# A two-layer hybrid decoder trunk: the operands of its Strassen products are prepared later in VectorE's queue, and its first weight is rounded earlier in ScalarE's

## The chip, the cores and the metric

The kernel runs on one core of one Trainium2 chip. TensorE (PE) multiplies matrices, VectorE (DVE) and ScalarE (ACT) work on rows of 128 partitions, GpSimd (POOL) does a few additions and subtractions, and SyncE (SP) and ScalarE issue the DMAs. The metric is the device time of one execution in microseconds (us); lower is better. Times are medians of the runs shown.

## The reference

Two pre-norm layers over 512 positions of width 1024, and a final norm. Each layer computes, from the normed input, a stick-breaking attention (four heads), a dilated attention (three groups of four heads, with partial rotary), two gates, merges the two branches and projects; then a gated feed-forward block with a convolution of width 3 follows. Cut to what the change touches:

```
h = rms_norm(x, norm_mix)                        # x: 512 x 1024
u = h @ w_in                                     # q, k, v of both attentions, and the gates
# stick-breaking, per head, t = query, s = key:
z = (q @ k.T) / 8
log_keep = where(s < t, log_sigmoid(-z), 0)
suffix   = reverse_cumsum(log_keep) - log_keep
A = where(s < t, exp(log_sigmoid(z) + suffix), 0)
yb = A @ v
# dilated attention: three groups (window, dilation), merged by their softmax denominators
```

## The kernel before

**Precision and weights.** Every float32 product is made of three products of rounded halves: with `hi` the rounded and `lo` the rest, `hi*h + hi*l + lo*h`. The weights stream in from memory in tiles `raw` of 512 KB (L290, issued by SyncE, five buffers); ScalarE writes `hi` (L299) and VectorE `lo = raw - hi` (L300) into a ring of twelve buffers. The same is done for activations: `xh` (L218) and `xl` (L219) for the normed input, `Bh` (L374) and `Bl` (L375) for the right operands below. Squares of x (L229, L232) serve the norm's root mean square, which is applied after the projections as `r` (`rbc`) or `rt` (`ny`).

**A layer's first part.** In this order of the program: the norm's splits and squares; a value projection, `vproj` (L344, four accumulators `acc` in PSUM, evicted by ScalarE at L347); the stick-breaking q and k, `sb_qk` (L320 to L322; each has two halves, so there are four evictions `sbq` in a layer, by VectorE, L591); a second, late value projection, whose four results ScalarE evicts into `stg` (L347) and eight DMAs on ScalarE's queue and eight on SyncE's scatter by residue (L352). All of these share four `acc` banks, so a projection cannot start before an older result in its bank is evicted. Then comes the stick-breaking attention itself, `sb_pair` (`z`, `e`, `sp`, `sh`: L500 to L538), mixed with the dilated projections.

**Right operands and Strassen products.** The dilated projections and the gates use a seven-product scheme of the Strassen kind on halves of the matrices. `hx` (L611, VectorE, eight times) scales x in place by the gain and the norm. `b_ops` then forms the operands named "11", "1", "2", "3", "21", "22" and "4": sixteen differences of half tiles on POOL (L405, written to `x` or to `T`), each split by ScalarE into `Bh` and by VectorE into `Bl`, and the four lower tiles split as they are (`plain`, 512 wide). `strassen` adds and subtracts blocks of a weight on POOL and VectorE (POOL: L427, L430, L440; VectorE: L431) and multiplies. The first product goes to a bank X, which ScalarE evicts as p1 into `s` (L429) before the fifth product may go on in X:

```
sprod(X, wsplit(a11), BT, "11", True)
S.activation(p1, X, AF.Copy)                 # L429
...
sprod(Y, wsplit(a11), BT, "2", True)
sprod(Z, wsplit(S1), BT, "1", True)
sprod(W, wsplit(a21), BT, "3", True)
sprod(X, wsplit(a12), BT, "21", False)
```

**What sets the order.** The program is written as above, but a scheduler places the instructions on each engine by its own model of their times; each engine then runs its queue strictly in order. `tc.issue_after(ins)` adds to what is written in its block the condition that it stands behind `ins`.

Of the kernel before, what the change touches and what calls it, by code (L numbers as in the profile page):

```python
# [13 lines left out]
AF = mybir.ActivationFunctionType  # L14
ALU = mybir.AluOpType
# [6 lines left out]
KD = 8  # L22
# [94 lines left out]
def trunk(ctx: ExitStack, tc: tile.TileContext, xt_d, pos_d, cst_d, vec_d, w_d, out_d):  # L117
    nc = tc.nc
    V, S, G, PE = nc.vector, nc.scalar, nc.gpsimd, nc.tensor
# [95 lines left out]
    def norm_split(k, gcol, st):  # L215
        h, lo = bslot_r("xh"), bslot_r("xl")
        g = vec[:, gcol + k:gcol + k + 1]
        S.activation(h, x[k], AF.Copy, scale=g)  # L218
        V.scalar_tensor_tensor(lo, x[k], g, h.bitcast(F32), op0=ALU.mult, op1=ALU.subtract)  # L219
        st["x", k] = (h, lo)  # L220
# [4 lines left out]
    def sq_sum(k, st):  # L225
        a = st.setdefault("a", [])
        if k < 2:
            a.append(scratch("sqa"))
            S.activation(a[k], x[k], AF.Square)  # L229
        else:  # L230
            q = temp("sq", tag="ta")
            S.activation(q, x[k], AF.Square)  # L232
            (V if k % 2 else G).tensor_tensor(a[k % 2], a[k % 2], q, ALU.add)  # L233
# [20 lines left out]
        V.scalar_tensor_tensor(y, t, 1.5, y, op0=ALU.add, op1=ALU.mult)  # L254
        return y

    last_row, last_num, last_out = [None], [None], [None]
    last_b = []

    def r_rows(y, n):  # L260
# [15 lines left out]
    def wraw(what, between=None):  # L276
        l, i = divmod(wpos[0], len(plan))
        wpos[0] += 1
        assert plan[i][0] == what
        n, out = plan_cols(plan[i]), []  # L280
        for c in range(0, n, 1024):
            e = min(n, c + 1024)
            raw = wp.tile([128, 1024], F32, tag="raw", name=nm("raw"), bufs=NRAW)
            o = int(offs[i]) + c
            if between and c == 0:
                nc.sync.dma_start(raw[:, :512], w_d[l, :, o:o + 512])
                between(0)
                nc.sync.dma_start(raw[:, 512:], w_d[l, :, o + 512:o + 1024])
            else:
                nc.sync.dma_start(raw[:, :e - c], w_d[l, :, o:o + e - c])  # L290
            if between:
                between(c // 1024 + 1)
            out += [raw[:, a:min(a + 512, e - c)] for a in range(0, e - c, 512)]
        return out, len(plan[i][1])

    def wsplit(src, n=512):
        hi = wp.tile([128, 512], F32R, tag="w", name=nm("hi"), bufs=NRING)
        lo = wp.tile([128, 512], F32R, tag="w", name=nm("lo"), bufs=NRING)
        S.activation(hi[:, :n], src, AF.Copy)  # L299
        V.tensor_tensor(lo[:, :n], src, hi[:, :n].bitcast(F32), ALU.subtract)  # L300
        return hi, lo

# [25 lines left out]
        V.tensor_tensor(lo, src, h.bitcast(F32), ALU.subtract)  # L328
        return h, lo

    def vproj(raw, xs, rt, evict, late=False):

        ps = [acc() for _ in range(4)]
        for k in range(KD):
            hi, lo = wsplit(raw[k])
            ops = [(b, k, x, w, x == 0 and w is hi) for x, w in ((0, hi), (1, hi), (0, lo)) for b in range(4)]
            if k == KD - 1 or late and k < 2:
                ops.sort(key=lambda o: o[0])
            if late and k == 0:
                held, ops = ops[9:], ops[:9]  # L340
            elif late and k == 1:
                ops = ops[:9] + held + ops[9:]
            for b, kk, x, w, first in ops:
                PE.matmul(ps[b], xs[kk][x][:, 128 * b:128 * b + 128], w, start=kk == 0 and first,  # L344
                          stop=kk == KD - 1 and x == 0 and not first)
        for b in range(4):
            S.activation(evict(b), ps[b], AF.Copy, scale=rt[:, b:b + 1])  # L347
# [194 lines left out]
    vcol = lambda l: l * NV  # L542
    st = {}
# [7 lines left out]
    first = wraw("in", load_x)  # L551
    nc.sync.dma_start(cst, cst_d)
    pos = temp("pos", I32, tag="ss")
    nc.sync.dma_start(pos[0:1], pos_d)
    for k in range(KD):
        norm_split(k, vcol(0), st)
        sq_sum(k, st)
    tri = one.tile([128, 128], F32R, name="tri")
# [15 lines left out]
    for l in range(L):  # L574
        b0 = vcol(l)
        c_ffn, c_bg, c_cw, c_cb = b0 + 8, b0 + 16, b0 + 32, b0 + 98
        xs = [st["x", k] for k in range(KD)]
        r, rt, rbc = rsq(st, pre)

        va, vb = ([vslot("v") for _ in range(4)] for _ in range(2))  # L580
        vproj((first or wraw("in"))[0], xs, rt, lambda b: va[b])
        first = None

        def sb_qk(sc, late):
            w = wchunk("in")
            o = []
            for m in range(2):
                ps = acc()
                proj(ps, w, xs, m)
                t = slot("sbq")  # L590
                V.scalar_tensor_tensor(t, ps, sc, r, op0=ALU.mult, op1=ALU.mult)  # L591
                o.append(t)
            return o

# [17 lines left out]
            return x[k]  # L612

        BT = {}
        for _ in b_ops(hx, BT):
            pass

        gqk = {}
        gv = [[t[:, 256:512] for t in va]] + [[t[:, 256 * g:256 * g + 256] for t in vb] for g in range(2)]
# [69 lines left out]
        for pr in range(2):  # L689
            a = slot("ya")  # L690
            for g in (1, 2, 0):
                ps = att("ub")
# [6 lines left out]
                n = num[g][pr]  # L699
                if g == 1:  # L700
                    V.tensor_tensor(a, ps, n, ALU.mult)
                else:
                    t = temp("t0", tag="ta")
# [66 lines left out]
        st = {}  # L770
        pre = preload(last_act)
        for m in range(KD):
            if m < 4:
                ps = first4[m]
            else:
                if m % 2 == 0:
                    w = wchunk("out")
                ps = acc()
# [4 lines left out]
        xs = [st["x", k] for k in range(KD)]  # L783
        r, rt, rbc = rsq(st, pre)

        BT = {}
# [36 lines left out]
        st, gs = {}, {}  # L823
        for what, g0, n, c in ffn_order():
# [12 lines left out]
            if g0 + n < MF:  # L837
                w = wchunk("dn")
                for j in range(2):
                    m = 2 * c + j  # L840
                    ps = att("dn")
# [7 lines left out]
            if l + 1 < L:  # L849
                for m in range(4 * c, 4 * c + 4):  # L850
                    ps = att("dn")
# [74 lines left out]
```

## Time and profile before

| what | value |
|---|---|
| median of three runs | 1427.2 us (1425.45 to 1427.45) |
| the profiled execution | 1426.62 us, span 1424.8 us |
| granted clock, mean | 0.994 |
| TensorE busy | 1396.4 us (98%) |
| VectorE busy | 1216.4 us (85%) |
| ScalarE busy | 804.2 us (56%) |
| POOL busy | 374.1 us (26%) |
| share of the chain that ended last | PE 76%, DVE 12%, issue 3%, ACT 2%, DMA 2%, POOL 1% |

The profiled execution lasts 1.8 us longer than its span, which counts from the first to the last instruction. TensorE is busy nearly all the time, so the other engines matter where TensorE waits for one of them. A matmul of 512 columns is shown with the time that it takes through the pipeline; the next one starts before it ends. The numbers behind names such as `acc` are left out in the trace.

### The profile page before, as it was taken

The page shows a single profiled execution, that of the slowest core. Times are in us where ns is not written, and L with a number is a line of the kernel's source. Part 1 is how long each engine was busy: PE and PEld are TensorE (multiplying, and loading weights), DVE is VectorE, ACT ScalarE, POOL GpSimd, SP SyncE. Part 2 cuts the span into 40 slices and gives each one's busy share as a digit, 9 for nine tenths or more (in the row PEclk, how much of TensorE's full clock was granted, in tenths as well). Part 3 has the DMA queues.
Part 4 walks back from the last instruction along what each step waited for, and adds up shares of the span by engine and source line. Part 5 has one row for each costly group of instructions (what it writes and reads, how often), then busy time and mean ns, then how long its engine had stood idle before and what let it go on. Part 6 is the DMA issues. An engine that isn't in the chain of part 4 may idle for free.

```text
span 1424.8 us, 24110 instructions
## 1 busy us (share of the span) xinstructions
PE 1396.4 (98%) x9030; PEld 1236.5 (87%) x9030; DVE 1216.4 (85%) x1932; ACT 804.2 (56%) x1662; POOL 374.1 (26%) x260
## 2 busy tenths in 40 slices
PE   8999999999999999999999999999999999999997
PEld 6787889988889999999888787999888899999997
DVE  7869987896799999998875889788869999999886
ACT  6456656764565445544653666577455645545455
POOL 1624332101122332232042423230013232332210
PEclk9999999999999999999999999999999999999999
DMA  6222321253213322322532222122431223322331
GB/s 236 89 93 77 93 81 60 75 171 110 75 60 113 110 89 102 122 101 78 178 104 88 98 81 74 63 89 90 163 101 62 89 89 102 122 89 91 110 96 60
DMA packets 44343, 141.55 MB, mean 99 GB/s; under 512 B 6337, under 2 KB 8513, under 8 KB 44226
## 3 DMA queue, kind: packets, MB, share of 16 engines
q1 hardware_dynamic: 41650, 135.69, 28.7%
q10 hardware_dynamic: 2576, 4.32, 0.8%
q8 instruction: 71, 1.16, 0.3%
q14 instruction: 46, 0.38, 0.1%
HBM read 130.55 MB, written 4.19 MB: 95 GB/s over the span
## 4 chain that ended last, share of the span: by engine, by line
PE 76%; DVE 12%; issue 3%; ACT 2%; DMA 2%; POOL 1%; ACTq 0%; SPq 0%; DVEq 0%; POOLq 0%
PE acc L418 11%; PE acc L416 11%; PE acc L417 11%; PE dn L321 5%; PE dn L320 5%; PE dn L322 5%; DVE lo L300 5%; PE acc L344 4%; PE acc L320 3%; PE acc L321 3%; PE acc L322 3%; PE qk L461 2%; PE num L484 1%; PE pv L538 1%; PE acc L753 1%
## 5 line engine op out<-in xcount | busy, mean ns | idle before, releaser
L299 ACT ACTIVATE hi<-raw 128x512 fp32r<-128x512 f32 x604 | 369.3, 623 | 315.7 <-DVE raw L431 70.8
L300 DVE TENSOR_TENSOR lo<-raw,hi 128x512 fp32r<-128x512 f32 x604 | 476.8, 796 | 69.9 <-ACT hi L299 58.3
L416 PE MATMUL acc<-Bh,hi 128*128 128x256 f32 x1792 | 513.5, 287 | 4.0 <-ACT hi L299 2.5
L417 PE MATMUL acc<-Bl,hi 128*128 128x256 f32 x1792 | 510.7, 285 | 0.0
L418 PE MATMUL acc<-Bh,lo 128*128 128x256 f32 x1792 | 509.3, 286 | 0.1
L416 PEld LDWEIGHTS acc<-Bh,hi 128*128 128x128 f32 x1792 | 343.6, 192 | 11.8 <-ACT hi L299 2.9
L417 PEld LDWEIGHTS acc<-Bl,hi 128*128 128x128 f32 x1792 | 343.9, 192 | 5.1 <-issue 2.8
L418 PEld LDWEIGHTS acc<-Bh,lo 128*128 128x128 f32 x1792 | 343.0, 192 | 2.3 <-issue 1.0
L427 POOL TENSOR_TENSOR ss<-raw 128x512 f32<-128x512 f32 x64 | 103.1, 1611 | 626.6 <-DMA raw<-in_w_dram 495.0
L320 PE MATMUL dn<-gh,hi 128*128 128x512 f32 (+1 forms) x376 | 141.3, 379 | 2.3 <-ACT hi L299 1.2
L322 PE MATMUL dn<-gh,lo 128*128 128x512 f32 (+1 forms) x376 | 140.8, 376 | 0.2 <-DVE lo L300 0.2
L321 PE MATMUL dn<-gl,hi 128*128 128x512 f32 (+1 forms) x376 | 141.0, 377 | 0.0
L440 POOL TENSOR_TENSOR raw<-raw 128x512 f32<-128x512 f32 x64 | 104.7, 1637 | 110.0 <-DVE lo L300 110.0
L430 POOL TENSOR_TENSOR raw<-raw,raw 128x512 f32<-128x512 f32 x64 | 104.2, 1628 | 3.2
L320 PEld LDWEIGHTS dn<-gh,hi 128*128 128x128 f32 x376 | 70.6, 189 | 15.0 <-ACT hi L299 2.1
L322 PEld LDWEIGHTS dn<-gh,lo 128*128 128x128 f32 x376 | 70.7, 188 | 13.7 <-DVE lo L300 1.1
L321 PEld LDWEIGHTS dn<-gl,hi 128*128 128x128 f32 x376 | 70.9, 189 | 11.3
L322 PE MATMUL acc<-xh,lo 128*128 128x512 f32 x192 | 75.2, 392 | 0.0
L321 PE MATMUL acc<-xl,hi 128*128 128x512 f32 x192 | 74.8, 390 | 0.0
L320 PE MATMUL acc<-xh,hi 128*128 128x512 f32 x192 | 74.7, 391 | 0.0
L233 POOL TENSOR_TENSOR sqa<-sqa,sq 128x512 f32<-128x512 f32 x12 | 16.6, 1383 | 201.4 <-ACT sq L232 201.4
L818 ACT ACTIVATE cv<-cv 128x512 f32<-128x512 f32 x44 | 27.8, 631 | 63.4 <-DVE cv L817 62.8
(216 smaller groups left out, 2309.0 us busy)
## 6 DMA issues: line engine op xcount, KB each, us to landing
raw<-in_w_dram SPq DMA_DIRECT2D x227, 512.0 KB, 3.7
x<-in_xt_dram SPq DMA_DIRECT2D x7, 512.0 KB, 5.5
raw<-in_w_dram SPq DMA_DIRECT2D x8, 384.0 KB, 3.8
x_dram<-x ACTq DMA_DIRECT2D x4, 512.0 KB, 2.7
x<-x_dram SPq DMA_DIRECT2D x4, 512.0 KB, 4.7
raw<-in_w_dram SPq DMA_DIRECT2D x6, 256.0 KB, 2.6
rot<-qk SPq DMA_DIRECT2D x48, 32.0 KB, 1.9
qk<-rot SPq DMA_DIRECT2D x48, 32.0 KB, 2.0
```

The costliest lines, as they stand in the source:

```text
L299: S.activation(hi[:, :n], src, AF.Copy)
L300: V.tensor_tensor(lo[:, :n], src, hi[:, :n].bitcast(F32), ALU.subtract)
L320: PE.matmul(ps, a, h, start=k == 0, stop=False)
L321: PE.matmul(ps, a, lo, start=False, stop=False)
L322: last = PE.matmul(ps, b, h, start=False, stop=k == n - 1)
L344: PE.matmul(ps[b], xs[kk][x][:, 128 * b:128 * b + 128], w, start=kk == 0 and first, stop=kk == KD - 1 and x == 0 and not first)
L416: PE.matmul(ps, a[:, c], hi, start=start and k == 0, stop=False, skip_group_check=True)
L417: PE.matmul(ps, a[:, c], lo, start=False, stop=False, skip_group_check=True)
L418: PE.matmul(ps, b[:, c], hi, start=False, stop=k == 3, skip_group_check=True)
L427: G.tensor_tensor(S1, a21, a22, ALU.add)
L430: G.tensor_tensor(a21, a11, a21, ALU.subtract)
L440: G.tensor_tensor(a11, a12, a11, ALU.subtract)
```

## The change

Two edits. The program's first normed tile, its first weight split and its first square are now written in this order: norm split, weight split, and the square behind the weight's rounding. And all of `b_ops`, with `hx`, is written in a block that stands behind the layer's last `sbq` eviction. Nothing is computed otherwise, and the number of instructions that do work is the same on each engine.

```diff
--- before.py
+++ after.py
@@ -254,7 +254,7 @@
         V.scalar_tensor_tensor(y, t, 1.5, y, op0=ALU.add, op1=ALU.mult)
         return y
 
-    last_row, last_num, last_out = [None], [None], [None]
+    last_row, last_num, last_out, last_sbq, last_hi = [None], [None], [None], [None], [None]
     last_b = []
 
     def r_rows(y, n):
@@ -296,7 +296,7 @@
     def wsplit(src, n=512):
         hi = wp.tile([128, 512], F32R, tag="w", name=nm("hi"), bufs=NRING)
         lo = wp.tile([128, 512], F32R, tag="w", name=nm("lo"), bufs=NRING)
-        S.activation(hi[:, :n], src, AF.Copy)
+        last_hi[0] = S.activation(hi[:, :n], src, AF.Copy)
         V.tensor_tensor(lo[:, :n], src, hi[:, :n].bitcast(F32), ALU.subtract)
         return hi, lo
 
@@ -328,11 +328,11 @@
         V.tensor_tensor(lo, src, h.bitcast(F32), ALU.subtract)
         return h, lo
 
-    def vproj(raw, xs, rt, evict, late=False):
+    def vproj(raw, xs, rt, evict, late=False, split0=None):
 
         ps = [acc() for _ in range(4)]
         for k in range(KD):
-            hi, lo = wsplit(raw[k])
+            hi, lo = split0 if split0 and not k else wsplit(raw[k])
             ops = [(b, k, x, w, x == 0 and w is hi) for x, w in ((0, hi), (1, hi), (0, lo)) for b in range(4)]
             if k == KD - 1 or late and k < 2:
                 ops.sort(key=lambda o: o[0])
@@ -552,7 +552,11 @@
     nc.sync.dma_start(cst, cst_d)
     pos = temp("pos", I32, tag="ss")
     nc.sync.dma_start(pos[0:1], pos_d)
-    for k in range(KD):
+    norm_split(0, vcol(0), st)
+    split0 = wsplit(first[0][0])
+    with tc.issue_after(last_hi[0].ins):
+        sq_sum(0, st)
+    for k in range(1, KD):
         norm_split(k, vcol(0), st)
         sq_sum(k, st)
     tri = one.tile([128, 128], F32R, name="tri")
@@ -578,8 +582,8 @@
         r, rt, rbc = rsq(st, pre)
 
         va, vb = ([vslot("v") for _ in range(4)] for _ in range(2))
-        vproj((first or wraw("in"))[0], xs, rt, lambda b: va[b])
-        first = None
+        vproj((first or wraw("in"))[0], xs, rt, lambda b: va[b], split0=split0)
+        first = split0 = None
 
         def sb_qk(sc, late):
             w = wchunk("in")
@@ -588,7 +592,7 @@
                 ps = acc()
                 proj(ps, w, xs, m)
                 t = slot("sbq")
-                V.scalar_tensor_tensor(t, ps, sc, r, op0=ALU.mult, op1=ALU.mult)
+                last_sbq[0] = V.scalar_tensor_tensor(t, ps, sc, r, op0=ALU.mult, op1=ALU.mult)
                 o.append(t)
             return o
 
@@ -612,8 +616,9 @@
             return x[k]
 
         BT = {}
-        for _ in b_ops(hx, BT):
-            pass
+        with tc.issue_after(last_sbq[0].ins):
+            for _ in b_ops(hx, BT):
+                pass
 
         gqk = {}
         gv = [[t[:, 256:512] for t in va]] + [[t[:, 256 * g:256 * g + 256] for t in vb] for g in range(2)]
```

How the queues change, at three places. First VectorE in layer 0, around the last two `sbq` evictions (`Bl` from `T` or `x` are right operands, `lo` weights, L615 is `hx`). Before:

```order
L591 SCALAR_TENSOR_TENSOR sbq_459<-acc_434,rbc_189 128x512
L375 TENSOR_TENSOR Bl_1080<-T_1034,Bh_1079 128x256 x2
L300 TENSOR_TENSOR lo_549<-raw_490,hi_548 128x512
L375 TENSOR_TENSOR Bl_1088<-x_80,Bh_1087 128x256 x2
L375 TENSOR_TENSOR Bl_1096<-x_81,Bh_1095 128x256 x2
L300 TENSOR_TENSOR lo_565<-raw_492,hi_564 128x512
L591 SCALAR_TENSOR_TENSOR sbq_486<-acc_461,rbc_189 128x512
```

After the change:

```order
L595 SCALAR_TENSOR_TENSOR sbq_459<-acc_434,rbc_193 128x512
L300 TENSOR_TENSOR lo_549<-raw_490,hi_548 128x512
L300 TENSOR_TENSOR lo_565<-raw_492,hi_564 128x512
L595 SCALAR_TENSOR_TENSOR sbq_486<-acc_461,rbc_193 128x512
L615 SCALAR_TENSOR_TENSOR x_80<-x_80,vec,rbc_193 128x512 x2
L615 SCALAR_TENSOR_TENSOR x_81<-x_81,vec,rbc_193 128x512 x2
L615 SCALAR_TENSOR_TENSOR x_82<-x_82,vec,rbc_193 128x512 x2
L300 TENSOR_TENSOR lo_581<-raw_492,hi_580 128x512
L615 SCALAR_TENSOR_TENSOR x_83<-x_83,vec,rbc_193 128x512 x2
L375 TENSOR_TENSOR Bl_1037<-x_80,Bh_1036 128x256 x2
```

The splits `Bl`, which had begun long before this place, now all stand behind the last `sbq`, and so do the eight scalings of x, which before stood far ahead. In the program's layer 1 the same holds.

Second, ScalarE in layer 1, around the four `stg` evictions, their DMA issues and p1 (L429). Before:

```order
L299 ACTIVATE hi_9135<-raw_9073 128x512
L299 ACTIVATE hi_9152<-raw_9071 128x512
L347 ACTIVATE stg_8574<-acc_8442,ny_8119 128x512
L347 ACTIVATE stg_8576<-acc_8443,ny_8119 128x512
L352 DMA v_8138<-stg_8574 32x512
...
L352 DMA v_8140<-stg_8580 32x512
L509 ACTIVATE e_8605<-z_8599 128x128
L509 ACTIVATE e_8619<-z_8601 128x128
L429 ACTIVATE s_1894_9080<-acc_9075 128x256
L299 ACTIVATE hi_9170<-raw_9071 128x512
```

After the change:

```order
L374 ACTIVATE Bh_9022<-x_3651 128x256
L347 ACTIVATE stg_8574<-acc_8442,ny_8119 128x512
L374 ACTIVATE Bh_9042<-x_3653 128x512
...
L509 ACTIVATE e_8605<-z_8599 128x128
L509 ACTIVATE e_8619<-z_8601 128x128
L374 ACTIVATE Bh_9046<-T_8960 128x256 x2
L299 ACTIVATE hi_9170<-raw_9071 128x512
L510 ACTIVATE e_8605<-e_8605 128x128
L510 ACTIVATE e_8619<-e_8619 128x128
L374 ACTIVATE Bh_9054<-T_8961 128x256 x2
L299 ACTIVATE hi_9187<-raw_9073 128x512
L429 ACTIVATE s_1894_9080<-acc_9075 128x256
```

A `Bh` of the operands "3" (from `x_3651`) and a 512-wide one now stand ahead of the second `stg`, and between the DMA issues and p1 there are ten instructions instead of two.

Third, POOL in layer 1, the end of the sixteen differences (L405) and the first weight blocks. Before:

```order
L405 TENSOR_TENSOR T_8961<-x_3653,x_3651 128x256
L405 TENSOR_TENSOR x_3651<-x_3653,x_3651 128x256
L405 TENSOR_TENSOR T_8960<-x_3652,T_8960 128x256 x2
L405 TENSOR_TENSOR T_8961<-x_3653,T_8961 128x256 x2
L427 TENSOR_TENSOR ss_9079<-raw_9073 128x512
L430 TENSOR_TENSOR raw_9073<-raw_9071,raw_9073 128x512
L427 TENSOR_TENSOR ss_9213<-raw_9207 128x512
L430 TENSOR_TENSOR raw_9207<-raw_9205,raw_9207 128x512
L440 TENSOR_TENSOR raw_9071<-raw_9071 128x512
```

After the change:

```order
L405 TENSOR_TENSOR T_8961<-x_3653,x_3651 128x256
L405 TENSOR_TENSOR x_3651<-x_3653,x_3651 128x256
L405 TENSOR_TENSOR T_8960<-x_3652,T_8960 128x256
L430 TENSOR_TENSOR raw_9207<-raw_9205,raw_9207 128x512
L405 TENSOR_TENSOR T_8961<-x_3653,x_3651 128x256
L405 TENSOR_TENSOR x_3651<-x_3653,x_3651 128x256
L440 TENSOR_TENSOR raw_9071<-raw_9071 128x512
L405 TENSOR_TENSOR T_8960<-x_3652,T_8960 128x256
L405 TENSOR_TENSOR T_8961<-x_3653,T_8961 128x256 x2
```

The differences and the weight sums L427, L430 and L440 now alternate. The row that writes `x_3651` for the second time, behind L430, is the difference from which the `Bh` right ahead of the first `stg` above is made; thirteen L405, counted from the first, one L427 and one L430 stand up to there from the first L405 on.

## Rows read from the trace of the kernel before

**Rows 1.** Waits of TensorE (engine, line, releaser: us in total, times, longest):
```profile
PE acc L344 <- ACT hi L299: 6.2, 1, 6.2
PE z L517 <- ACT sh L515: 3.1, 2, 2.8
...
PE acc L344 <- DVE sbq L591: 2.3, 1, 2.3
```

**Rows 2.** Timeline of ScalarE, the start (start us, us, line, tiles, [idle before, releaser]):
```profile
4.40 0.63 ACT L229 ACTIVATE sqa<-x 128x512 f32<-128x512 f32 x1 [1.93 <-DMA x<-in_xt_dram]
4.93 0.71 ACT L218 ACTIVATE xh<-x,vec 128x512 fp32r<-128x512 f32 x1
5.54 0.61 ACT L299 ACTIVATE hi<-raw 128x512 fp32r<-128x512 f32 x1
```

**Rows 3.** Timeline of TensorE at the start:
```profile
6.21 2.08 PE L344 MATMUL acc<-hi,xh 128*128 128x512 f32 x4 [6.21 <-ACT hi L299]
```

**Rows 4.** Timeline of VectorE, layer 0, end of the stick-breaking projections:
```profile
59.72 1.98 DVE L375 TENSOR_TENSOR Bl<-x,Bh 128x256 fp32r<-128x256 f32 x4
...
62.22 0.68 DVE L591 SCALAR_TENSOR_TENSOR sbq<-acc,rbc 128x512 f32<-128x512 f32 x1
```

**Rows 5.** Windows (stretch: us, busy us and instructions by engine, PEclk, DMA), layer 0:
```profile
63.82:67.23 3.41, 3.41 (x10) 2.63 (x9) 2.50 (x4) 2.85 (x6) 0.32 (x1) 0.50 0.49 154
```

**Rows 6.** Timeline of TensorE, layer 1, behind the late value projection:
```profile
777.42 0.49 PE L500 MATMUL z<-sbq,sbq 64*128 64x128 f32 x4
...
783.83 0.39 PE L416 MATMUL acc<-Bh,hi 128*128 128x256 f32 x1
```

**Rows 7.** Timeline of ScalarE, layer 1, around the staged evictions:
```profile
775.49 1.37 ACT L347 ACTIVATE stg<-acc,ny 128x512 f32<-128x512 f32 x2 [0.90 <-PE acc L344]
...
777.53 5.48 ACTq L352 DMA_DIRECT2D v<-stg  x7
783.06 0.45 ACT L509 ACTIVATE e<-z 128x128 f32<-128x128 f32 x2 [4.84 <-DMA v<-stg]
783.39 0.39 ACT L429 ACTIVATE s<-acc 128x256 f32<-128x256 f32 x1
783.65 0.64 ACT L299 ACTIVATE hi<-raw 128x512 fp32r<-128x512 f32 x1
784.17 0.52 ACT L510 ACTIVATE e<-e 128x128 f32<-128x128 f32 x2
```

**Rows 8.** ScalarE L374 by form (busy us, mean ns | idle before):
```profile
L374 ACT ACTIVATE Bh<-T 128x256 fp32r<-128x256 f32 x32 | 12.0, 408 | 6.5 <-PE acc L344 3.3 <-POOL T L405 2.6 <-DVE T L405 0.6
```

**Rows 9.** Timeline of VectorE, layer 1:
```profile
726.66 5.39 DVE L611 SCALAR_TENSOR_TENSOR x<-x,vec,rbc 128x512 f32<-128x512 f32 x8 [0.55 <-DMA raw<-in_w_dram]
...
745.72 2.73 DVE L375 TENSOR_TENSOR Bl<-x,Bh 128x256 fp32r<-128x256 f32 x3
748.37 0.41 DVE L375 TENSOR_TENSOR Bl<-T,Bh 128x256 fp32r<-128x256 f32 x1
...
749.04 1.23 DVE L300 TENSOR_TENSOR lo<-raw,hi 128x512 fp32r<-128x512 f32 x1
...
755.76 0.69 DVE L591 SCALAR_TENSOR_TENSOR sbq<-acc,rbc 128x512 f32<-128x512 f32 x1 [1.59 <-PE acc L322]
...
791.12 3.42 DVE L300 TENSOR_TENSOR lo<-raw,hi 128x512 fp32r<-128x512 f32 x2
```

**Rows 10.** Timeline of POOL, layer 1:
```profile
732.47 2.73 POOL L405 TENSOR_TENSOR x<-x 128x256 f32<-128x256 f32 x1 [19.25 <-DVE Bl L375]
...
745.48 2.69 POOL L405 TENSOR_TENSOR T<-x,T 128x256 f32<-128x256 f32 x3
748.86 0.86 POOL L405 TENSOR_TENSOR T<-x,T 128x256 f32<-128x256 f32 x1 [0.69 <-DVE Bl L375]
754.87 1.29 POOL L427 TENSOR_TENSOR ss<-raw 128x512 f32<-128x512 f32 x1 [5.15 <-DMA raw<-in_w_dram]
...
800.52 1.29 POOL L427 TENSOR_TENSOR ss<-raw 128x512 f32<-128x512 f32 x1 [6.52 <-DMA raw<-in_w_dram]
```

## The prediction

> **What bounds the kernel now.** I read the waits of TensorE first, then the timeline around each wait that the change can touch, engine by engine, then the granted clock by windows. TensorE is busy for 98% of the span, so a change is worth only what it takes from TensorE's few waits or adds to them. Three waits of the list matter here [rows 1]: 6.2 us at the start for the first weight half `hi`, 2.3 us, once, for an `sbq` eviction, and 3.1 us in two waits of the stick-breaking `z` for `sh`, the longer one 2.8.
>
> At the start, ScalarE squares x (4.40), rounds xh (4.93), and only then rounds the first weight (5.54) [rows 2]; the first matmul follows at 6.21 [rows 3]. In layer 0 the last `sbq` eviction starts at 62.22; four `Bl`, 1.98 us from 59.72, stand in VectorE's queue ahead of it [rows 4], as do others before them. TensorE waits 2.3 us, and right behind, from 63.82 to 67.23, the granted clock is 0.50, the lower of its two levels (1.2 of 2.4 GHz) [rows 5]. That stretch did in 3.41 us what takes half of it at full clock, so it cost 1.7 us more. In layer 1 the last `sbq` ran at 755.76 and had waited for TensorE, not the other way round [rows 9]: no such stall there.
>
> The place that decides is what follows the late value projection. I call its end T: 777.42 in layer 1, where the first `z` runs [rows 6]. ScalarE there evicts four `stg`, issues eight DMAs until 783.0, runs two `e`, and then evicts the first Strassen product, p1, at 783.39 (T+6.0) [rows 7]. TensorE's fifth product, which accumulates into the bank that p1 empties, starts at 783.83 [rows 6], straight behind the four products before it. So p1 is already just in time: each us that it comes later is a us of TensorE. Layer 0 has the same queues.
>
> **The start.** ScalarE's square, 0.53 us from start to start, leaves the path of the first weight. Its replacement at the head, xh, reads a gain as well as x; the rows show no wait of its own for that gain, so the gain of time lies between 0.53 and nothing. I take 0.3. The square itself comes back later, before ScalarE's next wait, and costs nothing.
>
> **Layer 0, the stall removed.** Behind the change no `Bl` stands ahead of an `sbq`. The wait of 2.3 us goes, and with it the 1.7 us of clock: minus 4.0. What is late next is below.
>
> **Both layers, the right operands.** The whole preparation, eight scalings `hx`, all `Bh`/`Bl` and sixteen POOL differences, began in layer 1 at 726.66 [rows 9]; now its VectorE part begins behind the fourth `sbq`, which ends at 756.4, T-21.0. In the changed queue stand eight `hx` (5.39 us, 0.67 each) [rows 9] and a `lo` of the same width (0.7), beside L427 and L430 on POOL, which I let cost 0.9: the first `Bl` is written, and POOL can start, at T-13.7. Up to the difference that ends operand "3" (the second `x_3651`), POOL has 13 L405, one L427 and one L430. The 16 L405 of before took 17.25 us, from 732.47 to 749.72, 1.08 each [rows 10]. Three in a row beside `Bl`s took 2.69, 0.9 each [rows 10], and the `Bl`s beside them 0.91 each, against 0.41 alone [rows 9]: the two engines step together. A 512-wide `lo` beside POOL took 1.23 [rows 9]. The changed VectorE queue holds 16 narrow and 12 wide instructions over that stretch; weighted, a step is 0.57 x 0.92 + 0.43 x 1.2 = 1.04. Thirteen are 13.5, L427 at 1.29 [rows 10] and L430 at the same make 16.1: that difference ends at P = T+2.4. Bounds: at 0.75 a step, below every group of three quoted, 12.3 and P = T-1.4; at 1.2 a step and 1.7 for the two wide ones, 19.0 and P = T+5.3. I take 1.04, since the same sixteen instructions gave 1.08.
>
> The Trainium skill, "SBUF — State Buffer", section "Who interferes with whom", says that a VectorE instruction with two SBUF inputs and a GpSimd instruction that reads SBUF exclude each other for the whole instruction, and whichever comes second waits. The pairs at 0.91 agree with that [rows 9, 10]. By the rule alone every POOL step behind a wide VectorE instruction would be at the 1.2 end, which is the heavy rival below.
>
> ScalarE's queue is in order. The last `Bh` of "3" now stands right ahead of the first `stg`, and another `Bh`, 512 wide, between the first and second. So the `stg` evictions, at T-2.0 before [rows 7], wait for P, and TensorE's first product cannot have its bank until P+1. Behind P: `Bh` 0.4, the way from the first `stg` to the first `e`, 7.6 as before (775.49 to 783.06 [rows 7]), the wide `Bh` 0.5, and then, in place of the two `e` ahead of p1, ten instructions: two `e`, four `Bh` at 0.41 [rows 8], two `hi` (0.64 each) and two more `e` (0.52 for the pair) [rows 7], 3.4 in all, since they overlap by some 0.1 each. p1 starts at P+11.9 = T+14.3 instead of T+6.0: 8.3 us later. TensorE is idle for most of that, in pieces, and an idle piece of 2.3 us was followed by the half clock [rows 5]. I take 1.3 of the 1.7 us for it, since part of a slow stretch would fall into the next piece of waiting; between 0 and 3.4. So 9.6 us per layer.
>
> **Layer 1, the stall absorbed.** The 2.8 us for `sh` hang on POOL's L427 at 800.52, which had been idle 6.52 us for a weight DMA [rows 10]. That DMA is queued on SyncE behind L444 on VectorE, which stood behind two `lo` that took 3.42 us instead of 1.3 from 791.12 [rows 9], beside POOL. In the changed queue these `lo`, and POOL's work that held them, depend on weights that arrive some 6 us later (an estimate: they are freed by `lo` that now run ahead of p1, where before they ran behind it), while TensorE's products come 9.6 later. The wait shrinks by the difference, 3.6, which is more than it is; with its slow stretch it gives back 2.75 + 1.7 = 4.45. If the DMA moves with the products instead, it gives back nothing.
>
> **The sum.** Layer 0: -0.3 - 4.0 + 9.6 = +5.3. Layer 1: 9.6 - 4.45 = +5.15. Together +10.45 on the profiled execution's 1426.6 us (its span is 1424.8), which is 0.6 below the median shown: 1437.1, so 1437. An effect under 0.2%, 2.9 us, is what a measurement of this kernel cannot tell from no change.
>
> **Rivals.** (a) POOL is quicker, P at or before T-2.4. Then the `stg`s run as before and only p1's extra eight instructions count, 2.9 us a layer. Place: ScalarE between the DMA issues and p1. If the clock falls behind these waits as it did behind 2.3 us [rows 5], layer 0 is -4.3 + 2.9 + 1.7 = +0.3 and layer 1 2.9 + 1.7 - 4.45 = +0.15: 1427, no change. For it: the narrow POOL instruction has room below 0.9. Against: the 12 wide VectorE instructions that now share the stretch, and the low bound of P, T-1.4, is still later than T-2.4.
>
> (b) The other side, faster: the same early P, but the waits before p1 leave the clock alone or are shorter than 2.9. Then -4.3 + 2.9 + 2.9 - 4.45 = -2.95: 1423.7, and down to 1418 if ScalarE's extra instructions cover idle time in full (-4.3 - 4.45). It decides as soon as p1 is less than some 3 us late in both layers. For it: the layer 0 stall is real and surely goes. Against: the same as under (a).
>
> (c) Heavier, with POOL at the exclusive price, P = T+5.3: 11.2 us of delay and 1.7 of clock a layer, 12.9; +8.6 and +8.45, 1443.7. The layer 1 stall that does not go would add 4.45 to the forecast, 1441.5. For it: wide pairs at 1.23 [rows 9]. Against: the mean of 1.08 over sixteen [rows 10].
>
> **How the numbers follow.** The forecast has 0.60, (a) 0.13, (b) 0.14, (c) and the stall that stays 0.13. Slower by over 0.2% takes the forecast and (c), 0.73, less 0.01 for its lowest end: 0.72; within 0.2%, (a) and that end, 0.14; faster 0.14. The range leaves out the heaviest part of (c) and the lower part of (b): 1425 to 1442. The forecast alone lies between 1431 and 1441, from P between T and T+4.
>
> **What would show it.** Right: TensorE's list of waits loses the `sbq` and gains, in both layers, a wait for `stg` or the first operands near T and one for `s` (p1) near T+8 to T+14; ScalarE idles before the first `stg` for POOL's `x`; `hx` stands behind the fourth `sbq`; the first matmul stands at 5.9; the wait for `sh` in layer 1 is gone. Wrong: if `stg` starts at T-2 in either layer, POOL was quicker than 1.04 and (a) or (b) holds; if `z` still waits 2.8 us for `sh`, the absorption fails; if p1 is late but TensorE runs other products meanwhile, the delay was not TensorE's.

## The result, and the profile after

The changed kernel takes 1441.77 us (median of five runs, 1441.24 to 1442.15); the kernel before, run beside it, 1425.45 us (1424.50 to 1427.45). The ratio is 1.0109, with a 95% interval of 1.0098 to 1.0120: slower by 1.1%. The profiled execution has a span of 1439.5 us against 1424.8, so 14.7 us are to be found in the traces.

TensorE's waits in the changed kernel (engine, line, releaser: us in total, times, longest), to be read beside [rows 1]:

```profile
PE acc L416 <- ACT stg L347: 6.7, 2, 3.4
PE acc L344 <- ACT hi L299: 5.7, 1, 5.7
PE acc L416 <- ACT s L429: 4.6, 2, 2.3
PE acc L418 <- DVE lo L300: 3.0, 3, 1.3
PE z L517 <- ACT sh L515: 2.9, 4, 1.9
```

The wait for `sbq` is gone. Two pairs of waits are new, one of each pair in each layer: 3.4 us for `stg`, and 2.3 us for `s`, which is p1. The wait for `sh` has nearly as much in total as before (2.9 against 3.1), but it is spread otherwise: its longest, 1.9, is now in layer 0.

The start, ScalarE and then TensorE, beside [rows 2, 3]:

```profile
4.42 0.72 ACT L218 ACTIVATE xh<-x,vec 128x512 fp32r<-128x512 f32 x1 [1.94 <-DMA vec<-in_vec_dram]
5.05 0.61 ACT L299 ACTIVATE hi<-raw 128x512 fp32r<-128x512 f32 x1
5.57 0.62 ACT L229 ACTIVATE sqa<-x 128x512 f32<-128x512 f32 x1
```

```profile
5.71 2.07 PE L344 MATMUL acc<-hi,xh 128*128 128x512 f32 x4 [5.71 <-ACT hi L299]
7.58 1.91 PE L344 MATMUL acc<-hi,xl 128*128 128x512 f32 x4
9.29 1.91 PE L344 MATMUL acc<-lo,xh 128*128 128x512 f32 x4
```

The first matmul starts 0.50 us earlier. But the second and third group of four take 1.91 us each, at a spacing of 0.43, until 11.25 us, where the granted clock goes to 1.00; in the kernel before it does so at 9.21, and the third group, at 9.53, took 1.07. By 22 us of the span nothing is left of the half microsecond.

VectorE in layer 0, beside [rows 4]: the last `sbq` no longer has anything ahead of it, and `hx` follows.

```profile
55.75 0.69 DVE L595 SCALAR_TENSOR_TENSOR sbq<-acc,rbc 128x512 f32<-128x512 f32 x1 [1.59 <-PE acc L322]
56.36 4.05 DVE L615 SCALAR_TENSOR_TENSOR x<-x,vec,rbc 128x512 f32<-128x512 f32 x6
...
62.26 1.42 DVE L375 TENSOR_TENSOR Bl<-x,Bh 128x256 fp32r<-128x256 f32 x4
```

Layer 1, where T (the first `z` after the late value projection) is 785.46. VectorE, beside the first differences; POOL, beside [rows 10]; ScalarE, beside [rows 7]; TensorE, beside [rows 6]:

```profile
770.32 1.42 DVE L375 TENSOR_TENSOR Bl<-x,Bh 128x256 fp32r<-128x256 f32 x4
771.66 1.88 DVE L300 TENSOR_TENSOR lo<-raw,hi 128x512 fp32r<-128x512 f32 x3
```

```profile
770.81 4.91 POOL L405 TENSOR_TENSOR x<-x 128x256 f32<-128x256 f32 x3 [10.01 <-DVE Bl L375]
...
787.54 0.91 POOL L405 TENSOR_TENSOR x<-x,x 128x256 f32<-128x256 f32 x1
788.41 1.44 POOL L440 TENSOR_TENSOR raw<-raw 128x512 f32<-128x512 f32 x1
...
793.11 1.13 POOL L405 TENSOR_TENSOR T<-x,T 128x256 f32<-128x256 f32 x1 [0.96 <-DVE Bl L375]
```

```profile
787.61 0.42 ACT L374 ACTIVATE Bh<-T 128x256 fp32r<-128x256 f32 x1 [0.89 <-POOL T L405]
...
788.80 0.67 ACT L347 ACTIVATE stg<-acc,ny 128x512 f32<-128x512 f32 x1
789.37 0.62 ACT L374 ACTIVATE Bh<-x 128x512 fp32r<-128x512 f32 x1
...
791.97 3.88 ACTq L352 DMA_DIRECT2D v<-stg  x5
795.90 0.45 ACT L509 ACTIVATE e<-z 128x128 f32<-128x128 f32 x2 [4.18 <-DMA v<-stg]
...
797.76 0.71 ACT L374 ACTIVATE Bh<-T 128x256 fp32r<-128x256 f32 x2
...
798.90 0.37 ACT L429 ACTIVATE s<-acc 128x256 f32<-128x256 f32 x1
```

```profile
785.46 0.49 PE L500 MATMUL z<-sbq,sbq 64*128 64x128 f32 x4
...
789.52 0.58 PE L416 MATMUL acc<-Bh,hi 128*128 128x256 f32 x1 [3.35 <-ACT stg L347]
...
799.32 0.39 PE L416 MATMUL acc<-Bh,hi 128*128 128x256 f32 x1 [2.30 <-ACT s L429]
```

These rows show one chain. The first three POOL differences start at 770.81 (T-14.7). The first of them alone took 3.34 us, while VectorE ran three `Bl` and three 512-wide `lo` without a pause. The one that ends operand "3" ends at 788.45; I call this time P, here T+3.0. Its `Bh` is one of the two from 787.93, and right behind, at 788.80, comes the first `stg`: before, it came at T-1.9, now at T+3.3. TensorE's first product waits for it until 789.52. Then ScalarE issues DMAs until 795.9, does the ten instructions, and p1 starts at 798.90, T+13.4. In layer 0 the same points are T = 77.40, P = T+3.0, p1 = T+13.4.

Three stretches around these waits (columns as in [rows 5]); all have the granted clock of 0.50, one in layer 0 and two in layer 1:

```profile
82.93:86.34 3.41, 3.41 (x18) 3.41 (x18) 3.41 (x5) 0.73 (x2) 2.28 (x3) 0.50 0.55 192
789.49:792.90 3.41, 3.38 (x16) 3.38 (x17) 3.41 (x4) 2.23 (x4) 2.66 (x3) 0.50 0.33 113
799.73:803.14 3.41, 3.41 (x18) 3.41 (x18) 3.41 (x9) 1.35 (x4) 1.41 (x2) 0.50 0.84 262
```

**Where the 14.7 us are.** I set TensorE's work in both traces side by side, matmul for matmul by the amount of work done, and read by how much the changed kernel is behind (the table is worked out so; a plus is a loss).

| stretch | change, us |
|---|---|
| start, up to 22 us | +0.1 |
| layer 0, up to T: the `sbq` wait and its slow stretch | -4.0 |
| layer 0, T to the fifth product | +7.5 |
| layer 0, from there to its end | +4.5 |
| layer 1, T to the fifth product | +7.4 |
| layer 1, behind it: slow stretch +1.6, wait for `sh` gone -4.6, small waits +2.2 | -0.8 |
| sum | +14.7 |

The granted clock was 0.50 in one more stretch of 3.41 us of each kernel, at 420.85 us of the changed one and at 1115.12 of the one before. By the end of the products around them, these two places had moved the sums by +0.2 and -0.4 us.

The biggest piece behind the fifth product in layer 0 is a wait that layer 1 had before and layer 0 had not. POOL in the kernel before, then POOL and TensorE in the changed one:

```profile
102.69 1.44 POOL L427 TENSOR_TENSOR ss<-raw 128x512 f32<-128x512 f32 x1 [4.90 <-DMA raw<-in_w_dram]
```

```profile
106.62 1.29 POOL L427 TENSOR_TENSOR ss<-raw 128x512 f32<-128x512 f32 x1 [7.45 <-DMA raw<-in_w_dram]
...
109.24 0.45 POOL L529 TENSOR_TENSOR sp<-sp,sp 128x128 f32<-128x128 f32 x1
```

```profile
111.03 0.39 PE L517 MATMUL z<-sh,tri 128*128 128x256 f32 x1 [1.85 <-ACT sh L515]
```

POOL had waited 7.45 us for a weight DMA, so the sum `sp` (L529) behind it in its queue came late, and with it its rounding on ScalarE, the `sh` that stands behind that rounding, and `z`, by 1.85 us. The lateness alone does not make this wait: L427 starts 7.9 us later behind T than before (T+29.2 against T+21.4), hardly more than the 7.5 us by which TensorE itself is late. TensorE's queue differs too. Between T and this `z` stand 165 matmuls of the Strassen products, where 182 stood before; at 0.12 us each that is 2.0 us less to do in the meantime. In layer 1 of the changed kernel the same `z` starts at the same place behind T (T+33.8, in layer 0 T+33.6) and waits 0.2 us only: there TensorE had lost 1.6 us to the slow stretch behind p1 (799.73). What else is lost behind the fifth product in layer 0 are a wait of 0.9 us for `lo`, one of 0.64 for `sh`, and smaller pieces.

### The profile page after: what moved, and what is told of

Its sections match the earlier page's. It is cut to its first block, busy times and chain, and to the rows that moved or that the text cites. A ratio compares the mean times of both kernels' runs of the same rounds, so it can differ in the third digit from the quotient of the medians.

```text
span 1439.5 us, 24111 instructions
## 1 busy us (share of the span) xinstructions
PE 1400.7 (97%) x9030; PEld 1239.3 (86%) x9030; DVE 1213.8 (84%) x1932; ACT 806.2 (56%) x1662; POOL 377.2 (26%) x260
## 4 chain that ended last, share of the span: by engine, by line
PE 78%; DVE 12%; issue 3%; POOL 2%; ACT 2%; DMA 2%; ACTq 0%; SPq 0%; DVEq 0%; POOLq 0%
PE acc L416 12%; PE acc L417 12%; PE acc L418 12%; DVE lo L300 5%; PE dn L320 5%; PE dn L321 5%; PE dn L322 5%; PE acc L344 4%; PE acc L320 4%; PE acc L321 4%; PE acc L322 4%; PE qk L461 2%; PE num L484 1%; PE yp L320 1%; PE acc L758 1%
## 5 line engine op out<-in xcount | busy, mean ns | idle before, releaser
L300 DVE TENSOR_TENSOR lo<-raw,hi 128x512 fp32r<-128x512 f32 x604 | 469.2, 783 | 87.7 <-ACT hi L299 71.9
L427 POOL TENSOR_TENSOR ss<-raw 128x512 f32<-128x512 f32 x64 | 104.5, 1633 | 674.1 <-DMA raw<-in_w_dram 549.5
L440 POOL TENSOR_TENSOR raw<-raw 128x512 f32<-128x512 f32 x64 | 103.3, 1614 | 98.0 <-DVE lo L300 98.0
L430 POOL TENSOR_TENSOR raw<-raw,raw 128x512 f32<-128x512 f32 x64 | 104.4, 1632 | 2.9
L320 PEld LDWEIGHTS dn<-gh,hi 128*128 128x128 f32 x376 | 70.6, 189 | 14.3 <-ACT gh L327 1.4
L300 DVE TENSOR_TENSOR lo<-ss,hi 128x512 fp32r<-128x512 f32 x64 | 64.8, 1013 | 2.3 <-ACT hi L299 2.1
```

The source lines that it names most:

```text
L320: PE.matmul(ps, a, h, start=k == 0, stop=False)
L427: G.tensor_tensor(S1, a21, a22, ALU.add)
L430: G.tensor_tensor(a21, a11, a21, ALU.subtract)
L440: G.tensor_tensor(a11, a12, a11, ALU.subtract)
```

## The experiments

All are compared with the kernel before on the same chip. A negative per cent is faster. The edits are shown against the changed kernel, that of e12 against the kernel before. In e2, e3, e4, e8 and e10 the first edit is taken out too, which their cuts do not show; lines below that edit then have their old numbers, in e8 one more.

**e1: the first edit alone.**

```diff
-        with tc.issue_after(last_sbq[0].ins):
-            for _ in b_ops(hx, BT):
-                pass
+        for _ in b_ops(hx, BT):
+            pass
```

> Edit one alone: the first square behind the first weight's rounding, b_ops as before. My theory: nothing is gained. In the changed kernel the first matmul came 0.50 us earlier, but its matmuls stayed at the slow spacing until 11.25 us instead of 9.21, and the shift against before was back at +0.1 by 21 us. So 1425.5 to 1427 us, as before, within 0.5 us, and the same slow spacing beyond 10 us. Rival: the first edit gains its half microsecond when it stands alone (1425.0 or less, 0.5 below the kernel before), and the slow spacing at the start is a matter of chance.

Measured: 1428.76 us against 1426.88, +0.12% (interval +0.04 to +0.21). Nothing is gained, but not for the reason that I gave: the slow spacing ended at 8.81 us here, and up to the `sbq` wait TensorE was 0.8 us ahead of the kernel before. The loss is in layer 0, where the scheduler put the operands otherwise (VectorE, then TensorE):

```profile
61.61 1.95 DVE L375 TENSOR_TENSOR Bl<-x,Bh 128x256 fp32r<-128x256 f32 x4
63.48 0.68 DVE L595 SCALAR_TENSOR_TENSOR sbq<-acc,rbc 128x512 f32<-128x512 f32 x1
```

```profile
64.21 0.79 PE L344 MATMUL acc<-hi,xh 128*128 128x512 f32 x1 [3.69 <-DVE sbq L595]
```

The `sbq` wait grew from 2.3 to 3.7 us, with 6.8 us of half clock behind it instead of 3.4. So the edit has no fixed price: it changes what the scheduler does 55 us later. Over the fourteen profiles the slow spacing at the start ended anywhere between 8.8 and 12.5 us, with the edit (8.8 to 11.7) and without (9.0 to 12.5), so that part of my theory is not borne out.

**e2 and e3: the second edit in one layer only.**

```diff
-        with tc.issue_after(last_sbq[0].ins):
+        with tc.issue_after(last_sbq[0].ins) if l == 0 else nullcontext():     # e3: l == 1
```

> Edit two in layer 0 alone (b_ops behind the last sbq there), no first square. My theory, read from the shift of TensorE's work in the two traces: -4.0 for the sbq wait and its half clock, +7.5 up to the fifth product, +4.5 behind it, in all +8.1: 1433.5 to 1435. Rival 1: the +4.5 behind the fifth product is an effect of the two layers together; then +3.5, 1429 to 1430. Rival 2, the forecast as it stood: +5.3, 1431.

> Edit two in layer 1 alone, no first square. My theory: +7.5 up to the fifth product, +1.6 for a half clock behind it, -4.3 for the wait for sh that goes, +2 behind that: +6.4, 1432 to 1433. TensorE keeps the 2.3 us wait for sbq in layer 0. Rival: the forecast's +5.15, 1431, or, if the wait for sh in layer 1 had gone only because layer 0 moved too, +10.7, 1437.

Measured: e2 1434.51 us, +0.58% (+0.46 to +0.70), that is +8.3 us by the ratio; e3 1434.08, +0.57% (+0.45 to +0.69), +8.1 us. Each layer by itself costs some 8 us, and layer 0 does so although its `sbq` wait goes. A loss behind the fifth product is there in layer 0 alone, so it is no effect of the two layers together. But the parts of e2 are not those of my theory: side by side its profile lost 8.5 us from T to the fifth product and 3.3 behind it, in place of 7.5 and 4.5. That the total agrees is in part luck. e3 is 1.7 above my number, just within its interval. With e1, the parts add up to 1.27%, against 1.09% for the whole; the intervals cover that.

**e4: half of the operands behind the last `sbq`, layer 0.**

```diff
-        with tc.issue_after(last_sbq[0].ins):
-            for _ in b_ops(hx, BT):
+        ops = b_ops(hx, BT)
+        for _ in range(2):
+            next(ops)
+        with tc.issue_after(last_sbq[0].ins) if l == 0 else nullcontext():
+            for _ in ops:
                 pass
```

> Layer 0 alone, and only the second half of the operands (3, the plain ones and 4) behind the last sbq; hx, 11, 1 and 2 stay early; layer 1 and the first square as before. My theory: the price of the change is the late begin of a chain of 13 to 16 POOL steps, not the moving of Bl past sbq as such. With six steps left for behind the sbq (about 7 us of 21) the stg evictions keep their place, p1 comes at T+6, and the sbq wait with its half clock goes: -4, 1421.5 to 1423. Rival: any Bl behind the last sbq delays the stg and p1; then no gain, 1426 or more.

Measured: 1425.24 us against 1426.88, -0.12% (-0.21 to -0.02). `stg` keeps its place (T-1.9), so the rival falls; but only 1.7 us come of the 4.0. TensorE still waited 0.9 us for the last `sbq`, which would leave 3.1; the interval, 0.3 to 3.0 us, hardly holds that, and where the rest went was not followed.

**e8: e4, and the sine table's product behind the last `sbq` too.**

```diff
-        V.tensor_scalar(St, St, cst[:, C_SGN:C_SGN + 1], None, op0=ALU.mult)
+        with tc.issue_after(last_sbq[0].ins):
+            V.tensor_scalar(St, St, cst[:, C_SGN:C_SGN + 1], None, op0=ALU.mult)
```

> The kernel before, with two edges in layer 0: the second half of the operands (as in e4) and the sign product of the sine table (L206, which waited 2.65 us for ScalarE in VectorE's queue ahead of the third sbq) behind the last sbq. My theory: the 0.9 us that TensorE still waited for sbq in e4 are the table's; with it behind, the wait goes in full: 4.0 below before, 1421.5 to 1423.5. Rival: what is left of e4's wait is Bl beside POOL (0.9 to 1.1 each), and nothing changes against e4: 1424.5 to 1426.

Measured: 1424.75 us, -0.11% (-0.21 to -0.01), as e4: my theory of the table falls. TensorE still waited 0.8 us for the last `sbq`. VectorE in e8:

```profile
56.33 2.06 DVE L376 TENSOR_TENSOR Bl<-T,Bh 128x256 fp32r<-128x256 f32 x2 [0.92 <-ACT Bh L375]
58.31 2.38 DVE L301 TENSOR_TENSOR lo<-raw,hi 128x512 fp32r<-128x512 f32 x2
60.62 0.68 DVE L592 SCALAR_TENSOR_TENSOR sbq<-acc,rbc 128x512 f32<-128x512 f32 x1
```

What stands ahead of the last `sbq` (60.62) are two `Bl` at about 1 us each and two `lo` at 1.2, as beside POOL. That agrees with the rival.

**e5: `hx` and operand 11 stay early, in both layers.**

```diff
+        ops = b_ops(hx, BT)
+        for _ in range(1):
+            next(ops)
         with tc.issue_after(last_sbq[0].ins):
-            for _ in b_ops(hx, BT):
+            for _ in ops:
                 pass
```

> The changed kernel, but in both layers hx and the split of operand 11 stay where they were; only what follows (all sixteen differences, operands 1 to 4 and the plain ones) is behind the last sbq. My theory: of the time by which the differences end late, P = T+3, the eight hx and the four Bl ahead of them make 6.6 us. Without them P is T-3.6, no stg waits, p1 comes between T+6 and T+7.5, the sbq wait stays away: 1423 to 1426. Rival: what costs is that the differences run beside the late weights' splits and sums at all, whenever hx runs; then stg still waits 2 us or more and the time is 1433 or more.

Measured: 1422.29 us against 1426.73, -0.32% (-0.43 to -0.21). All splits but those of 11 stand behind the last `sbq`, the `sbq` wait is gone, and nothing waits for `stg`. But the expectation described the kernel wrongly: POOL's first twelve differences ran before the last `sbq`, since only VectorE's instructions are held by the edge and a difference needs no `Bl` but that of 11. Only the last four were behind. ScalarE in layer 1, where T is 774.67 in this trace:

```profile
772.73 1.37 ACT L347 ACTIVATE stg<-acc,ny 128x512 f32<-128x512 f32 x2 [0.89 <-PE acc L344]
...
780.72 0.39 ACT L429 ACTIVATE s<-acc 128x256 f32<-128x256 f32 x1
```

p1 comes 8.0 us behind the first `stg`, as before (7.9 [rows 7]).

**e9: only `hx` stays early.** This tells the two parts of e5 apart.

```diff
+        for k in range(KD):
+            hx(k)
         with tc.issue_after(last_sbq[0].ins):
-            for _ in b_ops(hx, BT):
+            for _ in b_ops(lambda k: x[k], BT):
                 pass
```

> The changed kernel with only the eight scalings hx moved back ahead; every split, that of operand 11 too, is behind the last sbq. In e5 POOL's first differences ran before the last sbq after all, since only VectorE's splits stand behind it; here the first difference, which overwrites a tile that the 11 split must have read, cannot. So this tells e5's two parts apart. My theory: POOL's whole chain takes 22 to 23 us beside VectorE, as in the changed kernel (62.75 to 86.18 in layer 0), and starts at T-20.5; it ends at T+1.6, and the Bh of its last difference stands ahead of stg: stg at T+2 to T+3, p1 at T+9.5 to T+10.5: 1430 to 1435. Rival: hx alone was the delay; without it the chain ends before T-2, stg keeps its place: 1422 to 1425, as e5.

Measured: 1430.43 us against 1425.90, +0.30% (+0.20 to +0.40). POOL, ScalarE and TensorE in layer 0, T = 77.31:

```profile
56.76 2.00 POOL L405 TENSOR_TENSOR x<-x 128x256 f32<-128x256 f32 x2 [2.74 <-DVE Bl L375]
...
77.80 1.10 POOL L405 TENSOR_TENSOR T<-x,T 128x256 f32<-128x256 f32 x1 [0.96 <-DVE Bl L375]
```

```profile
79.78 1.25 ACT L347 ACTIVATE stg<-acc,ny 128x512 f32<-128x512 f32 x2
...
86.96 0.39 ACT L429 ACTIVATE s<-acc 128x256 f32<-128x256 f32 x1
```

```profile
80.50 0.39 PE L416 MATMUL acc<-Bh,hi 128*128 128x256 f32 x1 [2.48 <-ACT stg L347]
```

The chain starts at T-20.6, ends at 78.9 (T+1.6, 22.1 us), `stg` comes at T+2.5 and p1 at T+9.65: all as the theory said (in layer 1 p1 comes at T+10.5). So what is late is POOL's chain as a whole, which starts with the 11 split, and not `hx` alone.

**e7: the differences on VectorE.**

```diff
-            for _ in b_ops(hx, BT):
+            for _ in b_ops(hx, BT, V):
```

> The changed kernel with the sixteen differences on VectorE instead of POOL, so that POOL and VectorE no longer run them in step. My theory: P is set by the price of 0.92 to 1.2 us that a POOL difference has beside VectorE; on VectorE alone a difference costs 0.33, the last one of 3 ends before T-3 although VectorE has 5 us more to do, stg keeps its place, p1 comes at T+7: 1424 to 1428. Rival: VectorE's queue as a whole is what is too long; then P stays behind T and the time is 1437 or more.

Measured: 1427.97 us, +0.11% (+0.03 to +0.20): by the two ratios 1.0% better than the changed kernel, some 14 us. VectorE and ScalarE in layer 0:

```profile
67.21 0.41 DVE L405 TENSOR_TENSOR x<-x,x 128x256 f32<-128x256 f32 x1
67.55 0.41 DVE L405 TENSOR_TENSOR T<-x,x 128x256 f32<-128x256 f32 x1
```

```profile
75.59 0.69 ACT L347 ACTIVATE stg<-acc,ny 128x512 f32<-128x512 f32 x1 [0.47 <-PE acc L344]
...
84.29 0.38 ACT L429 ACTIVATE s<-acc 128x256 f32<-128x256 f32 x1
```

A difference takes a third of a microsecond from start to start on VectorE, and the first `stg` is where it was (T-1.9). It gains no more than that since p1, at T+6.8 and T+7.0 against T+5.8 and T+6.0 in the kernel before, still makes TensorE wait 0.7 and 0.9 us, and a wait of 2.5 us for `sh` is back in layer 1, in this profile with 10.24 us of half clock from 806.75 on.

**e6: the changed kernel with all scatter DMAs issued by SyncE.**

```diff
-            (nc.sync if r % 2 else nc.scalar).dma_start(dst[r][32 * b:32 * b + 32], src[r::4])
+            nc.sync.dma_start(dst[r][32 * b:32 * b + 32], src[r::4])
```

> The changed kernel with all sixteen scatter DMAs of stg on SyncE's queue, so that ScalarE's eight issues no longer stand between stg and p1. My theory: ScalarE's issues are a part of p1's delay; p1 comes at P+6.2 = T+9.2 instead of T+13.4, TensorE's wait for s (2.3 us a layer) goes, the wait for stg (3.4 a layer) stays: -4.6, and up to 1.7 more where a slow stretch goes with it: 1435 to 1437.5. Rival: SyncE's queue is then 5 us longer, weight DMAs come later and TensorE waits for sh or lo instead: 1441 or more.

Measured: 1427.02 us, +0.01% (-0.08 to +0.10). I expected some 5 us of gain and got 14.7. TensorE's waits:

```profile
PE acc L416 <- ACT stg L347: 6.7, 2, 3.4
...
PE z L517 <- ACT sh L515: 0.7, 1, 0.7
```

The wait for `stg` stays, and that for `s` goes but for 0.5 us, as said, though p1 comes at T+11.0 and not at T+9.2. But the waits behind it go too (`sh` from 2.9 to 0.7), and so does what was lost behind the fifth product: against the changed kernel the profile gains 2.4 us from T to layer 0's fifth product and 5.5 behind it. To see how much of that belongs to the change, two more runs have the same edit.

**e12: the kernel before with that edit, and e11: e5 with it.**

> The kernel before with the scatter DMAs on SyncE's queue alone, nothing else. It tells how much of e6's 14.7 us and of e11's 4.2 us is worth the same without the changed operands. My theory: e11's gain is SyncE's order (a weight DMA now stands between two rotary DMAs instead of behind four) and ScalarE's free 5 us, neither of which needs the change; so about -4 here too, 1421 to 1423, and the layer 1 wait for sh (2.8) goes. Of e6's gain some 10 us then are the change's own lateness behind p1. Rival: it is worth something only where p1 is late or the operands early; then 1425 to 1427 here.

> e5 with the scatter DMAs on SyncE's queue alone. My theory: with p1 at T+6.3 TensorE waits only 0.2 us for it, so taking ScalarE's issues away gives at most 0.4 in all and what it gave in e6 was p1's lateness: 1421.5 to 1422.5. Rival: e6's gain came from the other order of SyncE's weight DMAs; then it comes here too, 1418 or less, or the longer SyncE queue costs, 1425 or more.

Measured: e12 1421.65 us against 1425.54, -0.31% (-0.41 to -0.21); e11 1418.04 against 1425.90, -0.62% (-0.75 to -0.50). So the edit is worth 4 us without the change, and the same 4 in e5: my theory for e11 falls, and the rival's first part holds. In SyncE's queue of e12 the weight DMAs now stand between the rotary ones, and the layer 1 wait for `sh` is gone from TensorE's list (one of 1.1 us for `sl` stands in its place):

```profile
790.15 1.17 SPq L362 DMA_DIRECT2D rot<-qk  x2
791.43 1.00 SPq L290 DMA_DIRECT2D raw<-in_w_dram  x2
792.52 1.15 SPq L362 DMA_DIRECT2D rot<-qk  x2
```

If the edit is worth the same 4 us in the changed kernel, the other 10 to 11 of e6's 14.7 are the change's own lateness: p1 comes 2.4 us earlier without ScalarE's issues ahead of it, and what followed from it does not follow. That split is not shown. In e12 the gain lies in layer 1; behind T of layer 0, where the kernel before had no long wait for `sh` to lose, its profile gains nothing. In e6 5.5 us are gained behind layer 0's fifth product, and there, too, SyncE's weight DMAs stand between the rotary ones. Whether the earlier p1 or the earlier weight DMA brought these 5.5 stays open.

**e10: e5 without the first edit.** 

> e5 without the first edit (the squares as in the kernel before). My theory: where no sbq stall follows, the first edit is worth what TensorE starts earlier, 0.4 to 0.5 us, if the slow spacing at the start ends at the same place in the mean: 1422.5 to 1423. Rival: the first edit is worth nothing or costs: 1422.3 or less.

Measured: 1423.28 us, -0.26% (-0.34 to -0.17), against -0.32% (-0.43 to -0.21) with it. That is above my 1422.5 to 1423, and not what the rival said. The edit may be worth 0.8 us here; the intervals overlap, so it stays open whether it is worth anything.

e11 beats both kernels: `hx` and operand 11 early, the other splits behind the last `sbq`, the square behind the first weight, and all scatter DMAs on SyncE.

## Why the prediction was right, and where its terms were off

The forecast was slower by 10.45 us; measured were 14.7 between the profiles and 16.3 between the medians. So 1441.77 us lies just inside the upper end of the range, above the 1431 to 1441 that the prediction gave the forecast by itself. It is next to the 1441.5 of the layer 1 stall that stays, which is chance: that stall went, and other terms made up for it. The mechanism of the forecast is what the trace shows, link by link: POOL's chain late, `stg` behind it in ScalarE's queue, p1 behind the DMA issues, TensorE waiting at both places in both layers. e9 then foretold four times of that chain within half a microsecond in a kernel that starts it 6 us earlier, and e5, where the chain starts early, has none of it.

- **The layer 0 stall**: -4.0 forecast, -4.0 found. What was left out is that the slow stretch is no fixed part of such a wait (last section).
- **P**: T+2.4 forecast, T+3.0 found in both layers. POOL started at T-14.7, 1.0 earlier than taken, and needed 17.6 us in place of 16.1. The first difference took 3.34 us, beside six VectorE instructions in a row, where the sum had 1.04; L427 and L430 took 1.74 and 1.72 in place of 1.29. The other differences ran at 0.92, and at 1.2 beside 512-wide `lo`, as the row of steps gave.
- **p1**: T+14.3 forecast, T+13.4 found. The way from the first `stg` to the `e` was 7.1 us instead of 8.1: three of ScalarE's eight issues now start ahead of the fourth `stg`, one before. The ten instructions took 3.0 instead of 3.4. So p1 was 7.4 us later than before, not 8.3.
- **The slow clock up to the fifth product**: +1.3 forecast on top of the delay. This step was mis-sized: TensorE waited for p1 anyway, so that slow products in that time (82.93 and 789.49) cost nothing. The stretch T to the fifth product lost 7.5 us a layer, clock and all, not 9.6.
- **Behind the fifth product, layer 0**: the sum had nothing there, +4.5 were found. This is the term that was missing. The prediction named the mechanism for layer 1 (a weight DMA behind products in SyncE's queue, POOL behind the DMA, `sh` behind POOL) and did not ask whether it would make the same wait in layer 0. It took TensorE's queue as given, too, and by the times above the 17 matmuls fewer ahead of that `z` account for the wait of 1.85 us; no run tests that by itself. The other pieces of the 4.5 were not traced to a cause.
- **Behind it, layer 1**: -4.45 forecast, -0.8 found. The wait for `sh` did go, but for 0.2 us, with its slow stretch (-4.6), as forecast. POOL's L427 came 6.1 us later behind T, as the 6 of the estimate; TensorE came to that `z` 9.0 us later, 7.4 up to the fifth product and 1.6 in a new slow stretch behind p1. Without that stretch, which the sum did not have, TensorE would have waited some 1.8 us there, as in layer 0 (an estimate from these times). Against the -4.6 stood the 1.6 us of the stretch, and small waits of 2.2 us.
- **The first edit**: -0.3 forecast; +0.1 in the trace, and between -0.8 and +1.7 us by itself (e10 against e5, and e1). It moves other work, and that outweighs it.

The two oversized terms (8.3 + 1.3 for 7.5) and the two undersized ones partly cancel: -4.2 against +8.2. That the forecast time was nearer than its terms is luck. The rule on VectorE and GpSimd excluding each other (the Trainium skill, "SBUF — State Buffer", section "Who interferes with whom") agrees with POOL's rows: a difference beside a narrow `Bl` took 0.92 us, one beside a 512-wide `lo` 1.2, and the one beside six VectorE instructions in a row 3.34. The heavy rival, which had every step at 1.2, did not come true, since most VectorE instructions in between are narrow.

## What to carry to other kernels

Moving work behind a late instruction on one engine moves the whole chain that starts with it, on all engines: look for the first instruction that a chain on another engine needs (here a split that must have read a tile before POOL overwrites it), and leave that one early. Then follow the chain to the next thing that stands behind it in an in-order queue, DMA issues on a computing engine among them: here seven of eight took 5.5 us of ScalarE's queue ahead of p1 [rows 7], and without them p1 came 2.4 us earlier (e6). And when a wait in one layer is explained, ask whether the change makes the same wait in the other.

## What the runs showed of the hardware that I had not expected

- The half clock does not follow a wait for sure. In e6 TensorE waited 3.37 us for `stg` in layer 0 and 3.36 in layer 1, in the same place of the program: no slow stretch followed the first, one of 3.41 us the second. In e9, with 2.48 us twice, it was the same. In e12 the `sbq` wait of 2.27 us stayed and had no slow stretch. Over all profiles, 16 of 22 waits of 2 us or more were met or followed by one within 1.5 us (the first wait, at the start, left out). Shorter waits had one too, but less often: the stretch at 420.85 of the changed kernel follows a wait of 1.24 us, and of 37 waits between 1 and 2 us (those ahead of the final norm left out) 11 were followed by one.
- The first slow spacing of a run ended between 8.8 and 12.5 us, for kernels with the same first matmul to within 0.7 us (5.68 to 6.36). It lasted 2.9 to 6.2 us. At half speed for up to 3.2 us longer, that alone would move the time by up to 1.6 us from run to run (an estimate).
- A POOL difference takes 0.74 to 0.75 us with VectorE idle (e5, layer 1) and 0.92 beside narrow `Bl`. Where VectorE runs without a pause POOL's waits longer than that: 3.34 us beside six VectorE instructions in the changed kernel, and 7.09 beside a run of fourteen in layer 0 of e5, from 59.18.
